# A conv read one input phase later, with two stack tiles, taps built on chip, and blocks moved behind the conv layer norm

## The chip, the cores and the metric

The kernel runs on one core of a Trainium2 chip. The metric is the device time of one execution in microseconds (us), as the median of the runs.

## What is computed

The reference is one inference step of two layers over 288 tokens (256 of a prompt, 8 x 4 of samples). Of a layer, cut to what matters here:

```python
z = x @ w_in                        # columns: u (S5), cv and cg (conv)
y5 = _s5(u, ...)                    # complex diagonal state-space scan, 64 groups
s5_out = gelu(y5) * sigmoid(gelu(y5) @ s5_w_glu)
c = cv * sigmoid(cg)                # GLU
c = causal_dwconv(c, width 31)      # depthwise, per channel; the last 30 rows are an output too
c = silu(layernorm(c))              # over the 1024 conv channels
x = layernorm(ALPHA * x + concat([s5_out, c]) @ w_out)
...                                 # ConvFFN and input embedding, each with a layer norm
```

## The kernel before, in words

Activations lie transposed: 128 channels on the partitions, 288 tokens along the free axis. All weights come as one stream of 128x128 blocks, in the order in which TensorE uses them (`layer_phases`), eight blocks to a unit of 512 KB. SP's queue loads units into four buffers; ScalarE copies each to `whi` (rounded), VectorE makes the remainder `wlo`. Every block is three matmuls of 288 columns (`run`, L373, L378, L379): hi x hi, hi x lo, lo x hi. `next_block` makes the two units that follow the current one ahead of time.

In the mixer of a layer, phase `u0` computes four of the eight S5 inputs u. Then come eight input phases `p0` to `p7` of 32 blocks, each for one chunk of 128 conv channels (its value and its gate). Phases `v0`, `v2` and `v7` of 16 blocks compute u4, u5 and u6; `vz` computes u7. Behind that stand `oc` (the conv half of w_out), `g` (the S5 GLU) and `os` (the other half of w_out).

The conv of chunk j goes this way. `ev` evicts value and gate, and `glu` (VectorE, L144 through a helper that records every VectorE operation) writes their product into `cbuf`, a tile with one buffer that GpSimd's queue has filled with the cached rows (L1117). `cbuf` is stored to a DRAM scratch (`cb_d`, L1138). `stack(j)` then loads the taps `cw` (L1077, 512 KB, mostly zeros: 32 diagonal blocks for each group of 32 channels) and four shifted copies of the chunk back from the scratch into the tile `stack` (L1082, 4 x 282 KB), and stores `cbuf` as output (L1084). `conv(j)` is 64 matmuls of 256 columns (L1107) and 64 of 32 columns (L1110) on 32x32 tiles with `stack` and `cw`. `stack`, `cw` and `cbuf` have one buffer each. Program order is p_j, conv(j-1), stack(j), v_j. GpSimd's queue holds the loads and stores of the conv, some S5 elementwise work (L890 to L940) and the stores of u, y and k of the S5 part; the loads that go with those stores are on SP's queue, between the weights.

The S5 work (`s5`) is a set of generators, stepped between blocks (`tick`). Their waits are lags in an estimate of TensorE's time (`pe_t`, `at`, `wait`), so they set places in program order and not times. For each chunk of eight groups it does: `make_e` (the matrix `em`, L819), `inject` (tile `bu`), a scan on VectorE, `project` (tile `y`), gelu, and two trips through DRAM (`ust`, `u`); `tm` is a matrix that is loaded from DRAM through `k_d`.

Behind `conv(7)`, which follows v7, come four `vz` blocks, then `ln_finish`: statistics on TensorE, a chain of small VectorE operations that ends in `ln_dg`, with the other twelve `vz` blocks as the fill beside it, and a broadcast matmul (L514). Then `c_norm`, `c_silu` and the splits into `xh` (L532) and `xl` feed `oc`, chunk by chunk. `acc_tile` hands out five PSUM banks in turn.

Of the kernel before, what the change touches and what calls it, by code (L numbers as in the profile page):

```python
# [20 lines left out]
DEPTH = 2  # L21
# [32 lines left out]
TICK = 2  # L54
U_LAG = 8000.0
BACK_LAG = 7000.0
LOAD_LAG = 8000.0
# [9 lines left out]
EV_GAP = 10  # L67
HALF_GAP = 6
NATIVE = 10
U_AT = {0: [4], 2: [5], 7: [6]}  # L70
U_END = 7
V_CUT = (0, 4)

# [22 lines left out]
def layer_phases():  # L96
    ph = [("u0", _order("w_in", range(4), range(KD), 4))]
    for j in range(CVC):
        ph.append((f"p{j}", _order("w_in", [8 + j, 16 + j], range(KD), 0)))
        if j in U_AT:  # L100
            ph.append((f"v{j}", _order("w_in", U_AT[j], range(KD), 0)))
    ph.append(("vz", _order("w_in", [U_END], range(KD), 0)))
    ph.append(("oc", _order("w_out", range(KD), range(8, KD), 4)))
    ph.append(("g", _order("s5_w_glu", range(8), range(8), 4)))
    ph.append(("os", _order("w_out", range(KD), range(8), 5)))
    for z, ms in enumerate(EPARTS[:3]):
        ph.append((f"e{z}", _order("pe_w", ms, range(PEK), 0)))
# [12 lines left out]
    ph.append(("pg", _order("pe_w_gate", range(KD), range(KD), 5)))  # L120
    return ph
# [36 lines left out]
class Core:  # L158
# [249 lines left out]
    def ln_acc(self, st, v, last=False):  # L408
# [4 lines left out]
        if i == 0:  # L413
            def mean():
                cps = self.ln_banks(st, 1)[0]
                nc.tensor.matmul(cps[:, :TOK], self.ones_1, v, start=True, stop=True)
                st["c"], st["s1"], st["s2"] = self.ln_tile("ln_c"), self.ln_tile("ln_s1"), self.ln_tile("ln_s2")
                nc.scalar.activation(st["c"], cps[:, :TOK], AF.Copy, scale=1.0 / P)
                st["v0"] = v

            def first():
                self.V.tensor_tensor(v, v, st["c"], OP.subtract)
                nc.scalar.activation(st["s2"], v, AF.Square)
            self.defer(st.get("mean", 2) if st["n"] == DM else MEAN, mean)
            self.defer(2, first)
            return
# [23 lines left out]
    def ln_finish(self, st, fill=None, keep=False, subs=()):  # L450
# [26 lines left out]
        def sub(n=1):  # L477
            while subs and n:
# [29 lines left out]
        y = w  # L508
        dg = self.lp.tile([TG, 3, TG], F32, tag="ln_dg", name="ln_dg", bufs=1)
        V.scalar_tensor_tensor(dg, self.ident[:TG, :TG].rearrange("p (o t) -> p o t", o=1).to_broadcast([TG, 3, TG]),  # L510
                               -1.0, y.rearrange("p (z o) -> p z o", o=1).to_broadcast([TG, 3, TG]),
                               op0=OP.mult, op1=OP.mult)
        fill(1)
        nc.tensor.matmul(b0[:, 8:8 + TOK], self.ones_1[:TG], dg.rearrange("p z t -> p (z t)"),  # L514
                         start=True, stop=True)
# [207 lines left out]

    def stack_tile(self, mp):
        return mp.tile([P, 4, STW], F32, tag="stack", name="stack", bufs=1)


    def s5(self, l, mp):
# [250 lines left out]
        def prep():  # L979
# [7 lines left out]
            for c in range(S5C):  # L987
                while state["i"] < c - 1:
                    yield None
                yield from make_e(*ge)  # L990
                state["e"] = c
                if c + 1 < S5C:
# [62 lines left out]
    def mixer(self, l, ph):  # L1055
        nc, a = self.nc, self.a
        V = self.V
        with self.tc.tile_pool(name="mx", bufs=1) as mp:
# [12 lines left out]
            cst = self.ln_begin(CVC * P)  # L1071
            stacks, cbuf = {}, {}

            def stack(j):
                cb, d = cbuf.pop(j)
                cw = mp.tile([P, 4, 8, 32], F32, tag="cw", name="cw", bufs=1)
                nc.gpsimd.dma_start(cw, a["convw"][l, j])  # L1077
                out = self.stack_tile(mp)

# [4 lines left out]
                nc.gpsimd.dma_start(a["convo"][l, j], cb)  # L1084
                stacks[j] = (out, cw)

# [13 lines left out]
            def conv(j):  # L1100
                st, cw = stacks.pop(j)
                o = self.acc_tile()
# [10 lines left out]
                self.ln_acc(cst, cvo[j], j == CVC - 1)  # L1113

            for j in range(CVC):
                cb = mp.tile([P, CBW], F32, tag="cbuf", name="cbuf", bufs=1)
# [5 lines left out]
                def ev(m, acc):  # L1122
# [17 lines left out]
                    self.defer(2, glu)  # L1140
                self.run(ph[f"p{j}"], self.xs, ev)
                if j:
                    conv(j - 1)
                while "done" not in part:
# [5 lines left out]
            vz = ph["vz"]  # L1150
            vsum = self.sums(vz)
            conv(CVC - 1)
            self.run(vz[V_CUT[0]:V_CUT[1]], self.xs, ev_u, vsum)
            self.flush()
            self.ln_finish(cst, lambda z: z and self.run(vz[V_CUT[1]:], self.xs, ev_u, vsum), keep=True)
            th = {}
# [8 lines left out]
            def c_silu(j):  # L1165
# [3 lines left out]
            self.lazy(self.pipeline(CVC, ((0, lambda j: self.ln_sub(cst, cvo[j])), (1, c_norm), (2, c_silu),  # L1169
                                          (3, lambda j: self.split_lo(8 + j, cvo[j], 0.5)))))  # L1170

            def xs_c(k):
# [36 lines left out]
    def load_p(self, l, mp):  # L1209
        nc = self.nc  # L1210
        self.phi = self.pp.tile([P, PEK, TOK], F32R, name="phi", tag="phi", bufs=1)
        self.plo = self.pp.tile([P, PEK, TOK], F32R, name="plo", tag="plo", bufs=1)
        p32 = mp.tile([P, PEK, TOK], F32, name="p32", tag="sw", bufs=4)
# [123 lines left out]
    def build(self):  # L1337
# [11 lines left out]
        self.ones_d = pp.tile([P, P], F32, name="ones_d")  # L1349
        self.ones_1 = pp.tile([P, P], F32, name="ones_1")  # L1350
        self.ident = pp.tile([P, P], F32, name="ident")
# [8 lines left out]
        nc.vector.memset(self.ones_d, 1.0 / DM)  # L1360
        nc.vector.memset(self.ones_1, 1.0)

        warm = self.lp.tile([P, 1], F32, tag="warm", name="warm", bufs=1)
        nc.scalar.activation(warm, self.ones_1[:, 0:1], AF.Silu)
        make_identity(nc, self.ident)
# [40 lines left out]
def _pack(inp):  # L1406
# [42 lines left out]
    def by_state(names, order):  # L1449
# [5 lines left out]
                        for n in ("state_s5_re", "state_s5_im")], 3)  # L1455
    cw = np.zeros((DEPTH, CVC, 4, 32, 4, 8, 32), np.float32)
    w = np.zeros((DEPTH, 32, CVC * P), np.float32)
    w[:, :CK] = f["conv_w"]
    w = w.reshape(DEPTH, 8, 4, CVC, 4, 32).transpose(0, 3, 2, 5, 4, 1)
    for i in range(32):  # L1460
        cw[:, :, :, i, :, :, i] = w[:, :, :, i]
    o["convw"] = cw.reshape(DEPTH, CVC, P, 4, 8, 32)
    cv = np.zeros((DEPTH, CVC, P, CBW), np.float32)
# [53 lines left out]
```

## Time and profile before

| | us |
|---|---|
| median of 3 runs (2837.29 to 2851.84) | 2843.62 |
| profiled execution | 2835.36 |
| its span, first to last instruction | 2833.5 |
| TensorE busy in the span | 2697.6 |
| VectorE busy | 1820.6 |
| ScalarE busy | 1353.0 |
| GpSimd busy | 303.7 |

The mean granted clock of TensorE over the span is 0.978. The rows further down come from views of the trace: busy time by stretch, waits by engine, the timeline, groups by tile or line. L144 is the line of the helper through which all VectorE operations go, so they are told apart by their tiles. Times in the rows count from the start of the span; layer 0's conv stage is at 61 to 289 us, layer 1's at 1465 to 1694.

### The profile page before, as it was taken

Reading aid. Unit: us, or ns where it says so; the run is one execution under the profiler, and the core shown is the slowest. Engines: PE = TensorE matmul, PEld = TensorE weight load, DVE = VectorE, ACT = ScalarE, POOL = GpSimd, SP = SyncE. Lnnn points to the kernel's source line nnn. Section 1 sums busy time; section 2 is a strip of 40 time slices with the busy share of each in tenths; the row PEclk is TensorE's granted clock in tenths of the full one; section 3 lists DMA queues with packets and bytes.
Section 4 is the critical chain, followed back from the end, with each engine's and each line's share of the span. In section 5 each row is a group of like instructions: output and inputs, shape, how many; then the busy total and the mean of one; then the engine's idle time right before and its main releaser. Section 6 shows DMA issues by size and latency. Waiting matters only on the chain. (4 is left out here: it accounts for less than half of the span.)

```text
span 2833.5 us, 57988 instructions
## 1 busy us (share of the span) xinstructions
PE 2697.6 (95%) x23696; PEld 2634.5 (93%) x23696; DVE 1820.6 (64%) x3049; ACT 1353.0 (48%) x2224; POOL 303.7 (11%) x923
## 2 busy tenths in 40 slices
PE   8887899999999999999998879999999999999997
PEld 7776899999999999999897769999999999999997
DVE  6862778664566446667777537886645664566686
ACT  3442547553455345536364334475534553455363
POOL 3441100100000000000124311010000000000000
PEclk9998999999999999999999989999999999999998
DMA  7977444455454554554468864444554545445543
GB/s 231 252 203 210 147 161 155 160 164 177 159 168 160 182 162 159 174 169 150 158 187 234 226 174 161 160 156 157 173 173 154 171 161 182 161 159 176 166 154 101
DMA packets 175609, 487.72 MB, mean 172 GB/s; under 512 B 37616, under 2 KB 61696, under 8 KB 175344
## 3 DMA queue, kind: packets, MB, share of 16 engines
q1 hardware_dynamic: 160832, 434.56, 47.8%
q0 software_dynamic: 14512, 49.47, 6.4%
q8 instruction: 186, 3.05, 0.4%
q14 instruction: 79, 0.65, 0.1%
HBM read 463.27 MB, written 20.68 MB: 171 GB/s over the span
## 5 line engine op out<-in xcount | busy, mean ns | idle before, releaser
L373 PE MATMUL acc<-xh,whi 128*128 128x288 f32 x4656 | 1390.1, 299 | 14.5 <-ACT xh L532 8.1
L378 PE MATMUL acc<-xl,whi 128*128 128x288 f32 x4325 | 1280.7, 296 | 5.8 <-DVE xl L144 5.3
L379 PE MATMUL acc<-xh,wlo 128*128 128x288 f32 x4325 | 1275.3, 295 | 0.2 <-DVE wlo L144 0.2
L199 ACT ACTIVATE whi<-wraw 128x1024 fp32r<-128x1024 f32 x766 | 792.0, 1050 | 401.1 <-PE acc L378 237.7
L144 DVE TENSOR_TENSOR wlo<-wraw,whi 128x1024 fp32r<-128x1024 f32 x766 | 918.1, 1222 | 45.5 <-ACT whi L199 31.8
L373 PEld LDWEIGHTS acc<-xh,whi 128*128 128x128 f32 x4656 | 877.4, 188 | 20.5 <-ACT xh L532 9.0
L378 PEld LDWEIGHTS acc<-xl,whi 128*128 128x128 f32 x4325 | 814.8, 188 | 10.7 <-DVE xl L144 7.9
L379 PEld LDWEIGHTS acc<-xh,wlo 128*128 128x128 f32 x4325 | 818.0, 189 | 0.5 <-DVE wlo L144 0.5
L373 PE MATMUL acc<-hh,whi 128*128 128x288 f32 x1408 | 416.8, 296 | 0.0
L144 DVE SCALAR_TENSOR_TENSOR fo<-fe,parf,fo 128x304 f32<-128x304 f32 x352 | 188.1, 534 | 354.8 <-ACT fo L1253 348.5
L378 PE MATMUL acc<-hl,whi 128*128 128x288 f32 x1312 | 388.1, 296 | 0.0
L379 PE MATMUL acc<-hh,wlo 128*128 128x288 f32 x1312 | 387.7, 296 | 0.0
L373 PEld LDWEIGHTS acc<-hh,whi 128*128 128x128 f32 x1408 | 265.1, 188 | 0.1
L379 PEld LDWEIGHTS acc<-hh,wlo 128*128 128x128 f32 x1312 | 247.5, 189 | 0.0
L378 PEld LDWEIGHTS acc<-hl,whi 128*128 128x128 f32 x1312 | 247.2, 188 | 0.0
L1249 ACT ACTIVATE fe<-acc 128x256 f32<-128x256 f32 x176 | 67.5, 384 | 308.6 <-PE acc L379 308.6
L1259 POOL COPY fstage<-fe 128x9 f32<-128x9 f32 x176 | 41.8, 237 | 1069.1 <-ACT fe L1250 1064.3
L144 DVE TENSOR_TENSOR x<-x,acc 128x288 f32<-128x288 f32 x96 | 43.3, 451 | 151.3 <-PE acc L379 151.3
L432 ACT ACTIVATE ln_q<-x 128x288 f32<-128x288 f32 x90 | 40.2, 446 | 189.8 <-DVE x L144 189.8
L1253 ACT ACTIVATE fo<-fe,parf 128x304 f32<-128x304 f32 x176 | 112.9, 642 | 17.1 <-ACT fe L1250 0.7
L1107 PE MATMUL acc<-stack,cw 128*32 128x256 f32 x1024 | 79.9, 432 | 40.8 <-DMA stack<-cb_d 35.9
L1273 ACT ACTIVATE hh<-fth 128x288 fp32r<-128x288 f32 x88 | 39.2, 445 | 162.7 <-DVE fth L144 162.7
(237 smaller groups left out, 2373.2 us busy)
## 6 DMA issues: line engine op xcount, KB each, us to landing
wraw<-in_wts_dram SPq DMA_DIRECT2D x776, 512.0 KB
stack<-cb_d POOLq DMA_DIRECT2D x56, 282.0 KB, 9.6
cw<-in_convw_dram POOLq DMA_DIRECT2D x16, 512.0 KB, 6.5
cbuf<-in_convi_dram POOLq DMA_DIRECT2D x16, 283.5 KB, 4.1
cb_d<-cbuf POOLq DMA_DIRECT2D x16, 283.5 KB, 3.4
out_dram<-cbuf POOLq DMA_DIRECT2D x16, 283.5 KB, 11.7
tm<-k_d SPq DMA_DIRECT2D x64, 64.0 KB
sbt<-in_s5b_dram SPq DMA_DIRECT2D x14, 256.0 KB
```

Source lines behind the costliest of these rows:

```text
L144: return f(out, *args, **kw)
L199: self.nc.scalar.activation(hi, self.raw[s], AF.Copy)
L373: nc.tensor.matmul(out, w[0], xh, start=first, stop=False)
L378: nc.tensor.matmul(out, w[0], xl, start=False, stop=False)
L379: nc.tensor.matmul(out, w[1], xh, start=False, stop=last)
L432: nc.scalar.activation(st["q"], v, AF.Square)
L1107: nc.tensor.matmul(o[32 * b:32 * b + 32, :SEQ], cw[:, b, k], st[:, b, 4 * k:4 * k + SEQ], start=(k == 0), stop=False, tile_position=(0, 32 ...
L1249: nc.scalar.activation(e[:, 2:2 + SEQ], acc[:, :SEQ], AF.Copy)
L1253: nc.scalar.activation(o[:, :w], e[:, 2:EW], AF.Identity, bias=self.prm("ffn_conv_b", m), scale=self.prm("ffn_conv_w2", m))
L1259: nc.gpsimd.tensor_copy(stage[:, z, :, 0], e[:, SEQ:EW:6])
L1273: nc.scalar.activation(hh[i], h, AF.Copy, scale=0.5)
```

## The change

Program order becomes p_j, conv(j-2), taps(j-1), stack(j), v_j: the conv of a chunk is read one input phase later. Odd chunks use a second stack tile, which lies in the same memory as phi and plo (needed only after the mixer). The taps are no longer loaded as 512 KB blocks: 16 KB of weights are loaded on SP's queue, and one GpSimd multiply with a 32x32 identity (`eye`) spreads them to `cw`. u4 and u5 are computed after p1 and p3. Setting "matrix em is ready" is put 3 us of estimated TensorE time later. `vz` runs its k in the order 8 to 15, 0 to 7 and is cut in four: four blocks before conv(7), two behind it, six as the fill of `ln_finish`, and four behind the layer norm's first two chunks of normalisation. `ln_dg` shares a tile with `ln_q`, and `ones_1` goes (its users scale by 2048, a power of two). `HALF_GAP`, the least distance in blocks between evictions in `oc` and `os`, goes from 6 to 4.

```diff
+E_LAG = 3000.0
-HALF_GAP = 6
+HALF_GAP = 4
-U_AT = {0: [4], 2: [5], 7: [6]}
+U_AT = {1: [4], 3: [5], 7: [6]}
-V_CUT = (0, 4)
+V_CUT = (4, 6, 12)
...
-    ph.append(("vz", _order("w_in", [U_END], range(KD), 0)))
+    ph.append(("vz", _order("w_in", [U_END], [*range(8, KD), *range(8)], 0)))
...
-        dg = self.lp.tile([TG, 3, TG], F32, tag="ln_dg", name="ln_dg", bufs=1)
+        dg = self.ln_tile("ln_q")[:TG].rearrange("p (z t) -> p z t", z=3)
...
-    def stack_tile(self, mp):
+    def big_tile(self):
+        return self.pp.tile([P, 4 * STW], F32R, tag="big", name="big", bufs=1)
+
+    def stack_tile(self, mp, j=0):
+        if j % 2:
+            return self.big_tile().bitcast(F32).rearrange("p (s w) -> p s w", s=4)
         return mp.tile([P, 4, STW], F32, tag="stack", name="stack", bufs=1)
...
                 yield from make_e(*ge)
-                state["e"] = c
+                self.at(E_LAG, lambda: state.update(e=c))
...
+            def load_w(j):
+                wts[j] = mp.tile([P, 32], F32, tag="cwt", name="cwt", bufs=2)
+                nc.sync.dma_start(wts[j], a["convt"][l, j])
+
+            def taps(j):
+                if j + 1 < CVC:
+                    load_w(j + 1)
+                cws[j] = mp.tile([P, 4, 8, 32], F32, tag="cw", name="cw", bufs=1)
+                shp = [P, 32, 32]
+                nc.gpsimd.tensor_tensor(cws[j].rearrange("p b k o -> p (b k) o"),
+                                        wts.pop(j).rearrange("p (w o) -> p w o", o=1).to_broadcast(shp),
+                                        self.eye.rearrange("p (w o) -> p w o", w=1).to_broadcast(shp), OP.mult)
             def stack(j):
                 cb, d = cbuf.pop(j)
-                cw = mp.tile([P, 4, 8, 32], F32, tag="cw", name="cw", bufs=1)
-                nc.gpsimd.dma_start(cw, a["convw"][l, j])
-                out = self.stack_tile(mp)
+                out = self.stack_tile(mp, j)
...
+            load_w(0)
             for j in range(CVC):
...
                 self.run(ph[f"p{j}"], self.xs, ev)
+                if j > 1:
+                    conv(j - 2)
                 if j:
-                    conv(j - 1)
+                    taps(j - 1)
                 while "done" not in part:
                     self.late.pop(0)[1]()
                 stack(j)
...
+            conv(CVC - 2)
+            taps(CVC - 1)
+            self.run(vz[:V_CUT[0]], self.xs, ev_u, vsum)
             conv(CVC - 1)
             self.run(vz[V_CUT[0]:V_CUT[1]], self.xs, ev_u, vsum)
             self.flush()
-            self.ln_finish(cst, lambda z: z and self.run(vz[V_CUT[1]:], self.xs, ev_u, vsum), keep=True)
+            self.ln_finish(cst, lambda z: z and self.run(vz[V_CUT[1]:V_CUT[2]], self.xs, ev_u, vsum), keep=True)
...
+            self.need(1 - LOOK)
+            self.run(vz[V_CUT[2]:], lambda k: (self.xh[k], self.xl[k]), ev_u, vsum)
...
-        self.phi = self.pp.tile([P, PEK, TOK], F32R, name="phi", tag="phi", bufs=1)
-        self.plo = self.pp.tile([P, PEK, TOK], F32R, name="plo", tag="plo", bufs=1)
+        t = self.big_tile()
+        self.phi, self.plo = [t[:, i * PEK * TOK:(i + 1) * PEK * TOK].rearrange("p (k t) -> p k t", k=PEK)
+                              for i in range(2)]
```

## Rows read from the trace of the kernel before

**Rows 1.** Busy time by stretch: us, busy of each engine, granted clock, DMA share, GB/s.

```profile
61.00:289.17 228.17, 187.66 (x2970) 168.06 (x2970) 138.32 (x250) 85.99 (x158) 76.85 (x137) 0.92 0.80 225
...
360.00:1410.00 1050.00, 1045.60 (x7831) 1042.71 (x7830) 669.18 (x1043) 524.50 (x837) 49.48 (x275) 1.00 0.51 164
...
1464.60:1693.95 229.35, 186.75 (x2975) 167.11 (x2975) 136.12 (x253) 85.03 (x161) 73.74 (x138) 0.92 0.80 220
```

**Rows 2.** Waits of TensorE, 61 to 289: us in total, times, longest.

```profile
PE acc L1107 <- DMA stack<-cb_d: 17.3, 4, 8.1
PE bu L393 <- DMA tm<-k_d: 6.2, 1, 6.2
PE y L393 <- DMA tm<-k_d: 4.6, 1, 4.6
```

**Rows 3.** Waits of TensorE, 1465 to 1694.

```profile
PE acc L1107 <- DMA stack<-cb_d: 18.7, 4, 8.6
PE bu L393 <- ACT em L819: 9.2, 6, 5.5
```

**Rows 4.** Busy time by stretch: an input phase, a conv, a v phase, inject, project.

```profile
210.46:223.55 13.09, 13.04 (x103) 12.80 (x96) 4.46 (x7) 3.25 (x5) 3.30 (x6) 1.00 0.93 248
224.89:229.02 4.13, 4.13 (x129) 3.17 (x129) 1.23 (x1) 1.40 (x3) 1.09 (x2) 1.00 1.01 265
256.69:263.35 6.66, 6.65 (x57) 6.42 (x48) 3.84 (x6) 2.73 (x4) 1.07 (x2) 1.00 0.82 216
165.76:167.10 1.34, 1.34 (x65) 1.16 (x64) 1.34 (x3) 1.34 (x5) 0.00 (x0) 1.00 0.97 293
...
128.18:129.82 1.64, 1.64 (x98) 1.53 (x97) 1.64 (x2) 1.36 (x2) 1.64 (x4) 1.00 0.87 247
```

**Rows 5.** Timeline of VectorE and GpSimd, 229.5 to 256.6: start, us, instruction, [idle before].

```profile
230.47 0.53 DVE L144 SCALAR_TENSOR_TENSOR cbuf<-cvt 128x256 f32<-128x256 f32 x2 [4.28 <-DMA cbuf<-in_convi_dram]
...
255.08 0.53 DVE L144 SCALAR_TENSOR_TENSOR cbuf<-cvt 128x256 f32<-128x256 f32 x2 [9.95 <-DMA cbuf<-in_convi_dram]
...
235.18 2.20 POOL L1082 DMA_DIRECT2D stack<-cb_d  x4 [2.80 <-DMA cb_d<-cbuf]
...
251.78 0.56 POOL L1117 DMA_DIRECT2D cbuf<-in_convi_dram  x1 [13.85 <-DMA out_dram<-cbuf]
```

**Rows 6.** Tile cbuf on VectorE, 40 to 300: durations, first and last start.

```profile
L144 DVE SCALAR_TENSOR_TENSOR cbuf<-cvt x16: 180/324/469, 59.9 to 255.4; 128x256 f32<-128x256 f32 x8, 128x32 f32<-128x32 f32 x8
```

**Rows 7.** DMA issues of the page: count, KB each, median us to landing.

```profile
stack<-cb_d POOLq DMA_DIRECT2D x56, 282.0 KB, 9.6
cw<-in_convw_dram POOLq DMA_DIRECT2D x16, 512.0 KB, 6.5
...
out_dram<-cbuf POOLq DMA_DIRECT2D x16, 283.5 KB, 11.7
```

**Rows 8.** A GpSimd and a VectorE multiply by line or tile: ns min/median/max.

```profile
L895 POOL TENSOR_TENSOR sd<-keep,mag x32: 656/667/1649, 49.9 to 1721.3; 128x288 f32<-128x288 f32 x32
...
L144 DVE TENSOR_TENSOR sw<-sqb,sbt x16: 680/684/1476, 40.9 to 1702.6; 128x512 f32<-128x512 f32 x16
```

**Rows 9.** Busy time by stretch: conv 7, and from its end to the first oc block.

```profile
274.92:289.17 14.25, 10.23 (x85) 9.51 (x78) 8.57 (x26) 7.09 (x14) 1.32 (x3) 1.00 0.25 83
...
269.46:274.92 5.46, 5.46 (x129) 3.45 (x129) 0.00 (x0) 0.00 (x0) 0.00 (x0) 0.74 0.83 306
```

**Rows 10.** Timeline of VectorE and ScalarE in the conv layer norm.

```profile
279.79 0.16 DVE L144 TENSOR_SCALAR ln_ne<-acc 96x6 f32<-96x6 f32 x1 [3.75 <-PE acc L463]
...
282.32 0.46 DVE L144 SCALAR_TENSOR_TENSOR ln_dg<-ident,ln_n 96x288 f32<-96x288 f32 x1
...
291.54 0.43 ACT L532 ACTIVATE xh<-cvo 128x288 fp32r<-128x288 f32 x1
```

**Rows 11.** Waits of TensorE, 289 to 360 (oc).

```profile
PE acc L373 <- ACT xh L532: 4.0, 1, 4.0
PE acc L378 <- DVE xl L144: 3.7, 2, 2.9
```

More of the change, by code (lines that the diff above doesn't have):

```diff
@@ L415, in mean @@
                 cps = self.ln_banks(st, 1)[0]
-                nc.tensor.matmul(cps[:, :TOK], self.ones_1, v, start=True, stop=True)
+                nc.tensor.matmul(cps[:, :TOK], self.ones_d, v, start=True, stop=True)
                 st["c"], st["s1"], st["s2"] = self.ln_tile("ln_c"), self.ln_tile("ln_s1"), self.ln_tile("ln_s2")
-                nc.scalar.activation(st["c"], cps[:, :TOK], AF.Copy, scale=1.0 / P)
+                nc.scalar.activation(st["c"], cps[:, :TOK], AF.Copy, scale=float(DM) / P)
                 st["v0"] = v
@@ L508, in ln_finish @@
         y = w
-        dg = self.lp.tile([TG, 3, TG], F32, tag="ln_dg", name="ln_dg", bufs=1)
+        dg = self.ln_tile("ln_q")[:TG].rearrange("p (z t) -> p z t", z=3)
         V.scalar_tensor_tensor(dg, self.ident[:TG, :TG].rearrange("p (o t) -> p o t", o=1).to_broadcast([TG, 3, TG]),
-                               -1.0, y.rearrange("p (z o) -> p z o", o=1).to_broadcast([TG, 3, TG]),
+                               -float(DM), y.rearrange("p (z o) -> p z o", o=1).to_broadcast([TG, 3, TG]),
                                op0=OP.mult, op1=OP.mult)
         fill(1)
-        nc.tensor.matmul(b0[:, 8:8 + TOK], self.ones_1[:TG], dg.rearrange("p z t -> p (z t)"),
+        nc.tensor.matmul(b0[:, 8:8 + TOK], self.ones_d[:TG], dg.rearrange("p z t -> p (z t)"),
                          start=True, stop=True)
@@ L1071, in mixer @@
             cst = self.ln_begin(CVC * P)
-            stacks, cbuf = {}, {}
+            stacks, cbuf, cws, wts = {}, {}, {}, {}
+            def load_w(j):
[9 more added lines that the diff above has]
+                                        self.eye.rearrange("p (w o) -> p w o", w=1).to_broadcast(shp), OP.mult)
             def stack(j):
                 cb, d = cbuf.pop(j)
-                cw = mp.tile([P, 4, 8, 32], F32, tag="cw", name="cw", bufs=1)
-                nc.gpsimd.dma_start(cw, a["convw"][l, j])
-                out = self.stack_tile(mp)
+                out = self.stack_tile(mp, j)
                 def back(eng):
@@ L1084, in stack @@
                 nc.gpsimd.dma_start(a["convo"][l, j], cb)
-                stacks[j] = (out, cw)
+                stacks[j] = out
             def window(t, b, off):
@@ L1100, in conv @@
             def conv(j):
-                st, cw = stacks.pop(j)
+                st, cw = stacks.pop(j), cws.pop(j)
                 o = self.acc_tile()
@@ L1349, in build @@
         self.ones_d = pp.tile([P, P], F32, name="ones_d")
-        self.ones_1 = pp.tile([P, P], F32, name="ones_1")
         self.ident = pp.tile([P, P], F32, name="ident")
@@ L1360, in build @@
         nc.vector.memset(self.ones_d, 1.0 / DM)
-        nc.vector.memset(self.ones_1, 1.0)
         warm = self.lp.tile([P, 1], F32, tag="warm", name="warm", bufs=1)
-        nc.scalar.activation(warm, self.ones_1[:, 0:1], AF.Silu)
+        nc.scalar.activation(warm, self.ones_d[:, 0:1], AF.Silu)
         make_identity(nc, self.ident)
@@ L1455, in _pack @@
                         for n in ("state_s5_re", "state_s5_im")], 3)
-    cw = np.zeros((DEPTH, CVC, 4, 32, 4, 8, 32), np.float32)
     w = np.zeros((DEPTH, 32, CVC * P), np.float32)
@@ L1459, in _pack @@
     w = w.reshape(DEPTH, 8, 4, CVC, 4, 32).transpose(0, 3, 2, 5, 4, 1)
-    for i in range(32):
-        cw[:, :, :, i, :, :, i] = w[:, :, :, i]
-    o["convw"] = cw.reshape(DEPTH, CVC, P, 4, 8, 32)
+    o["convt"] = w.reshape(DEPTH, CVC, P, 32)
     cv = np.zeros((DEPTH, CVC, P, CBW), np.float32)
```

## The prediction

> **What bounds the kernel now.** I read the stretches first [rows 1]. Behind the conv stage TensorE is busy 1045.6 of 1050 us: there nothing but fewer matmuls would help, and the change takes none away. The two conv stages (61 to 289 and 1465 to 1694) are another matter: 187.7 of 228.2 and 186.8 of 229.4 us busy, at a mean granted clock of 0.92. So 40.5 and 42.6 us stand idle, and part of the busy time runs at 1.2 instead of 2.4 GHz.
>
> The waits of TensorE name the idle time [rows 2, 3]: the stack reload is first in both stages (17.3 and 18.7 us, in four waits each), then the S5 transfers (6.2 and 4.6) and, in layer 1, the matrix `em` (9.2 in six waits).
>
> How much is work? I price the pieces from undisturbed stretches [rows 4]: an input phase of 32 blocks 13.0 us, a conv chunk 4.1, a `v` phase 6.6, an S5 chunk 1.3 + 1.6 = 3. Seven phases, three `v`, the 16 blocks of `vz` (as a `v`), eight convs and six S5 chunks are 91 + 20 + 6.6 + 33 + 18 = 169, with some 4 for the layer norm's matmuls 173. The stage takes 228: 55 us per layer are lost, 40.5 as idle time and the rest to the half clock behind it. That is all that the change can win, about 107 us in two layers.
>
> A second chain runs beside TensorE. `cbuf` has one buffer: GLU j writes it, it goes to DRAM, comes back as the stack, is stored as output, and only when that store has landed may GpSimd's queue load the next `cbuf`, for which GLU j+1 waits on VectorE. One round [rows 5]: GLU at 230.47, stack loads issued at 235.18, next `cbuf` load at 251.78, next GLU at 255.08 after VectorE sat idle for 9.95 us: **24.6 us a round**. TensorE needs 17.1 for such a chunk. From the first GLU to the last are 195.5 us [rows 6], 27.9 per chunk.
>
> **The change part by part.**
>
> *Conv one phase later, two stack tiles.* The stack of j is loaded after p_j as before, but read after p_(j+2) instead of p_(j+1): 17 us more for a load that PE waited for 8 us at most. Its waits (36.0 in both layers [rows 2, 3]) go to zero, but for the last chunk. What is late next is the `cbuf` round, which this part doesn't touch.
>
> *Taps on chip.* Out go 16 loads of 512 KB from GpSimd's queue; 16 loads of 16 KB on SP's queue come in, one phase ahead. In a round that queue moves 512 + 4 x 282 + 2 x 283.5 = 2207 KB [rows 7] in the 21.3 us from GLU to `cbuf` load [rows 5], so 512 KB are 4.9 us of it at this pace; the bounds are 0 (the load runs while the GLU store is still on its way) and 6.5, its whole time to landing [rows 7]. I take 4, nearer to the pace: a round of 20.6.
>
> In come 16 GpSimd multiplies of 128x1024. The nearest rows are 128x288, 0.667 us median and 1.649 at most [rows 8]: by elements 2.4 to 5.9 us. Each waits for the end of conv j-2 (its one `cw` tile), as the load did; behind it in the queue stand the stack loads of j and the S5 stores. The multiply lies in the 4.7 us between GLU and stack issue [rows 5], so I cost its queue time at nothing; without that cover it is 2.4 to 5.9 a round. VectorE can lose time too: its two-input 128x512 multiply takes 0.684 at the median and 1.476 at most [rows 8]. VectorE is busy for 138 of 228 us [rows 1]; bounds 0 and 8 x 5.9 = 47 per layer, I take 3, near the lower end, since wlo is built two units ahead. The Trainium skill ("SBUF — State Buffer", Who interferes with whom) says that a VectorE instruction with two SBUF inputs and a GpSimd one that reads SBUF shut each other out for a whole instruction. The largest values of rows 8 look like that; the rule's price is in a rival.
>
> *Sum up to the last GLU.* TensorE's chunks in the new order, from p_j to p_(j+1), are 16.0 (p, S5), 22.6 (v1), 20.1 (conv 0), 26.7 (conv 1, v3), 20.1, 20.1 and 17.1: 142.7. Seven rounds of 20.6 are 144. The later of the two, chunk by chunk (TensorE to chunk 4, 85.4, then three rounds, 61.8, and 2 for eviction and GLU), gives about 150. On top I keep the S5 transfer waits (10.8 [rows 2]) and 4 for half clock after them: 165 instead of 195.5, a gain of 30.5 per layer.
>
> *E_LAG.* The injection is put 3 us later in TensorE's queue, so other blocks fill the waits for `em`. These waits are not kept in the sum above. The S5 chain has room: VectorE is far from full. Putting u4 and u5 one phase later moves S5 chunks 4 and 5 into phases where VectorE idles; no cost.
>
> *Tail and layer norm.* GLU 7 to conv 7 took 14.4 us (255.08 to 269.46 [rows 5, 9]). Now conv 6 and four `vz` blocks stand in between, and the taps of 7 are built only after conv 6: 2.4 to 5.9 us against a cover of 1.6. With less in the queue I take 14 (12 to 17). Conv 7 takes 4.1 rather than 5.46 at a clock of 0.74 [rows 4, 9]. From its end to the first w_out block were 14.25 us [rows 9]. Two blocks fewer before the statistics, 0.8; the fill falls from 12 blocks to six, 2.5 us, and the VectorE chain that it covers takes 3.0 (279.79 to 282.78 [rows 10]): 2.4 less fill and 0.5 of new wait, 1.9; the last four blocks lie in the 4.0 us wait for `xh` [rows 11]. So 11.6, a gain of 2.7. The tail gains 0.4 + 1.4 + 2.7 = 4.5.
>
> Two costs. `ev_u` of `vz` now stands in ScalarE's queue behind the first normalisations, and the second w_out accumulator takes its bank: the third `xh` ended at 291.97 [rows 10], 2.8 us after w_out's start, so a wait of about 3 there; but this phase is held by VectorE later anyway (3.7 us of `xl` waits [rows 11]), so it hides. S5 chunk 6 comes 4 us sooner relative to w_out and meets that VectorE jam: 2. `HALF_GAP`, `ln_dg` in `ln_q`, `ones_1`, phi and plo in the large tile: nothing on the path.
>
> Per layer: 30.5 + 4.5 - 3 - 2 = 30; two layers 60. The profiled execution took 2835.4 us (span 2833.5) and becomes about 2775; the median of the runs shown lies 8.3 above the profiled one. 2843.6 - 60 = **2784**; with kept waits of 5 to 25 instead of 15, 2764 to 2804.
>
> **The rivals.**
> 1. *The cbuf round keeps its length.* The load left out was hidden in the GLU store's flight, and 24.6 us hold: 7 x 24.6 + 2 + 8 of waits = 182, gain 13.5 + 4.5 - 5 = 13 per layer: 2818. For it: VectorE waits 9.95 us for `cbuf` already [rows 5]. Against: the stack pieces stand behind the 512 KB in one queue. The Trainium skill ("DMA: Bandwidth & Descriptors", Anatomy of one DMA) has about 2 us and bytes by 436 GB/s for a GpSimd DMA: by that 512 KB in the queue are 1.2 us, the round 23.4 and the time, as an estimate, 2802. No run here shows it; the pace above is four times slower.
> 2. *The round shrinks by 6.5 and everything else hides*: TensorE alone sets the pace, 142.7 + 2 + 4 = 149, gain 46.5 + 4.5 - 1 = 50: 2744. Against: DMA share 0.80 over the stage [rows 1], and S5 waits that no edit addresses.
> 3. *The multiply locks VectorE.* If each holds VectorE for its 2.4 us and wlo is late by that: 19 per layer instead of 3: 2816. For: the spread of rows 8. This is the rule on shared ports as a mechanism of this kernel. Against: slack of two units.
> 4. *The wait moves into the queues.* SP and GpSimd loads have lags in estimated TensorE time; with fewer stalls they get less real time, and S5 transfers are awaited for 20 us more per layer: 2824. For: 10.8 us of such waits now.
> 5. *Slower.* The multiply falls behind the GLU store and takes 5.9 us of every round, with no relief from the load left out: 30.5 x 7 = 213.5 against 195.5, with 5 of VectorE and 4.5 of tail gain 18.5 lost per layer: 2880. It decides from 3.3 us a round in which GpSimd is not hidden (27.9 - 24.6). Against: the median row gives 2.4.
>
> That the change doesn't do what it says, is not likely: one tile less to wait for is plain in the order of instructions.
>
> **How the numbers follow.** Forecast 0.44, rival 1 0.20, rival 2 0.13, rival 3 0.08, rival 4 0.09, rival 5 0.06. The range takes in the forecast with its bounds, rivals 1, 3 and 4 and the upper part of 2: 2750 to 2826. A measurement of this kernel can tell some 0.5% (14 us) from no change: faster than 2829 holds for the first five cases but a part of 1 and 4 (their own spread is some 10 us): faster 0.86, same 0.08, slower 0.06.
>
> **What would show it.** Stack waits of TensorE under 8 us in all, and only before conv 7; no `em` waits over 1 us; granted clock over 0.95 in both stages; first to last GLU 155 to 175 us, `cbuf` rounds of 19 to 22 where they bind; GpSimd multiplies of 2 to 5 us, inside the GLU store's flight; from conv 7's end to w_out under 13 us. I am wrong if VectorE waits for `cbuf` as long as before and wlo waits appear at TensorE (rivals 1, 3), or if waits for tm and ust grow (rival 4).

## The result and the profile after

The changed kernel takes 2812.5 us where the kernel before, on the same chip, takes 2842.8: a ratio of 0.9889 (0.9861 to 0.9916). The forecast was 2784, with 60 us of gain; about half of it came. The direction and the range (2750 to 2826) hold, the size does not. The profiled execution fell less than the median, from a span of 2833.5 to 2810.9 us, 22.6, and the trace is read against that.

The waits that were to go are gone. TensorE's waits in the whole profile after (us in total, times, longest):

```profile
PE bu L394 <- ACT em L825: 19.1, 10, 9.4
...
PE kps L863 <- DVE bsm L145: 11.4, 3, 5.7
PE y L394 <- ACT kp L868: 7.4, 1, 7.4
PE acc L376 <- DVE wlo L145: 6.8, 2, 4.5
...
PE acc L1125 <- POOL cw L1090: 3.7, 3, 3.2
PE acc L1125 <- DMA big<-cb_d: 3.3, 1, 3.3
```

The stack reload, 36.0 us before [rows 2, 3], costs 3.3, once, ahead of conv 7; the `tm` waits (10.8 [rows 2]) are no longer in the list. In their place stand four that wait for an engine and not for a transfer: `em`, `bsm`, `kp` and `wlo`, 44.7 us together, three of them operands of S5. The DMA issues of the page after say that the shorter queue is real, 9.6 and 11.7 us before [rows 7]:

```profile
stack<-cb_d POOLq DMA_DIRECT2D x32, 282.0 KB, 7.3
big<-cb_d POOLq DMA_DIRECT2D x24, 282.0 KB, 7.0
...
out_dram<-cbuf POOLq DMA_DIRECT2D x16, 283.5 KB, 9.9
```

The gain can be put in its place with the tile `cbuf` on VectorE (the GLUs; durations, first and last start), layer 0 and layer 1 of the kernel after:

```profile
L145 DVE SCALAR_TENSOR_TENSOR cbuf<-cvt x16: 182/297/628, 59.3 to 246.2; 128x256 f32<-128x256 f32 x8, 128x32 f32<-128x32 f32 x8
...
L145 DVE SCALAR_TENSOR_TENSOR cbuf<-cvt x16: 180/301/427, 1453.6 to 1642.6; 128x256 f32<-128x256 f32 x8, 128x32 f32<-128x32 f32 x8
```

First to last GLU is 186.9 and 189.0 us; before it was 195.5 [rows 6] and, in layer 1, 195.7. That is 8.6 and 6.7 us, where 30.5 a layer were forecast. From the last GLU to the first w_out block the time fell by 3.7 and 5.8 us, where 4.5 were forecast. So one term is missing, and it is the largest. A cut at the fifth GLU shows where. The first four chunks, before and then after (us, busy PE, PEld, DVE, ACT, POOL, granted clock, DMA share, GB/s):

```profile
59.90:181.80 121.90, 105.15 (x1889) 95.39 (x1893) 96.57 (x171) 51.81 (x98) 52.73 (x93) 0.94 0.85 240
1464.30:1583.30 119.00, 100.55 (x1732) 91.15 (x1734) 90.23 (x164) 50.15 (x97) 50.22 (x93) 0.93 0.85 233
```

```profile
59.30:177.30 118.00, 100.10 (x1635) 91.14 (x1637) 96.75 (x160) 49.08 (x92) 51.85 (x91) 0.93 0.82 228
1453.60:1574.90 121.30, 97.99 (x1643) 88.51 (x1645) 90.17 (x153) 49.68 (x96) 55.72 (x92) 0.92 0.74 211
```

The first four chunks gained nothing: 240.9 us before, 239.3 after. Nearly the whole gain of this term is in the last three rounds, from the fifth GLU to the last: 68.6 and 67.4 us, where the kernel before took 73.3 and 76.4.

### The profile page after: what moved, and what is told of

It reads as the page before. It is cut to its first block, busy times and chain, and to the rows that moved or that the text cites. A ratio compares the mean times of both kernels' runs of the same rounds, so it can differ in the third digit from the quotient of the medians.

```text
span 2810.9 us, 57976 instructions
## 1 busy us (share of the span) xinstructions
PE 2690.3 (96%) x23696; PEld 2623.7 (93%) x23696; DVE 1845.6 (66%) x3048; ACT 1352.4 (48%) x2224; POOL 325.8 (12%) x923
## 5 line engine op out<-in xcount | busy, mean ns | idle before, releaser
L379 PE MATMUL acc<-xl,whi 128*128 128x288 f32 x4325 | 1283.7, 297 | 12.9 <-DVE xl L145 12.6
L145 DVE TENSOR_TENSOR wlo<-wraw,whi 128x1024 fp32r<-128x1024 f32 x766 | 921.7, 1227 | 25.6 <-ACT whi L200 11.8
L145 DVE SCALAR_TENSOR_TENSOR fo<-fe,parf,fo 128x304 f32<-128x304 f32 x352 | 188.2, 535 | 345.3 <-ACT fo L1280 339.0
L1276 ACT ACTIVATE fe<-acc 128x256 f32<-128x256 f32 x176 | 67.4, 383 | 286.1 <-PE acc L380 286.1
L433 ACT ACTIVATE ln_q<-x 128x288 f32<-128x288 f32 x90 | 40.1, 446 | 189.9 <-DVE x L145 189.9
L145 DVE SCALAR_TENSOR_TENSOR x<-x,acc 128x288 f32<-128x288 f32 x64 | 28.9, 451 | 124.6 <-PE acc L380 124.6
```

Of the source, the lines that this page charges most:

```text
L145: return f(out, *args, **kw)
L379: nc.tensor.matmul(out, w[0], xl, start=False, stop=False)
L433: nc.scalar.activation(st["q"], v, AF.Square)
L1276: nc.scalar.activation(e[:, 2:2 + SEQ], acc[:, :SEQ], AF.Copy)
```

## Experiments

Two theories stood at the start. **Held queue**: GpSimd works its queue in order; the next `cbuf` load stands in it and waits there until the output store has landed (115.5 us in 14 waits after), and S5's small GpSimd operations, which are queued behind it, come late; ScalarE and VectorE pass that on to TensorE. **Full VectorE**: the multiply on GpSimd shuts VectorE out, and `wlo` and S5 come late for that. The hold in the kernel after:

```profile
POOL cbuf L1136 <- DMA out_dram<-cbuf: 115.5, 14, 12.0
```

The ratios all stand against the kernel before, run on the same chip; a difference of two ratios is uncertain by about 0.004 (10 us). `HALF_GAP`, the shared `ln_dg` tile, `ones_1` and the new order of `vz` were not tried one by one.

| kernel | median us | ratio (95%) | first to last GLU, us |
|---|---|---|---|
| after | 2812.5 | 0.9889 (0.9861 to 0.9916) | 186.9, 189.0 |
| after, store first | 2776.5 | 0.9784 (0.9757 to 0.9811) | 174.9, 175.1 |
| after, taps loaded | 2847.3 | 1.0030 (1.0013 to 1.0047) | 189.3, 194.0 |
| after, no E_LAG | 2810.2 | 0.9895 (0.9868 to 0.9923) | 189.0, 189.9 |
| after, layer norm as before | 2822.8 | 0.9948 (0.9928 to 0.9968) | 187.1, 197.4 |
| before, store first | 2817.4 | 0.9932 (0.9910 to 0.9955) | 193.3, 186.9 |
| before, taps built | 2811.3 | 0.9907 (0.9882 to 0.9932) | 184.6, 182.4 |
| after, store first, taps loaded | 2808.4 | 0.9898 (0.9877 to 0.9918) | 172.9, 182.6 |
| after, store first, short load | 2781.7 | 0.9803 (0.9772 to 0.9834) | 172.4, 174.5 |
| after, store first, multiply twice | 2797.4 | 0.9868 (0.9844 to 0.9893) | 182.3, 188.2 |
| before, taps built, store first | 2789.9 | 0.9825 (0.9799 to 0.9850) | 176.1, 174.3 |
| after, S5 blocks as before | 2807.9 | 0.9898 (0.9880 to 0.9916) | 188.0, 186.9 |
| after, conv order as before | 2797.0 | 0.9859 (0.9835 to 0.9883) | 186.8, 187.5 |

**The output store ahead of the stack loads** (on the kernel after).

```diff
-                back(nc.gpsimd if j < CVC - 1 else nc.sync)
                 nc.gpsimd.dma_start(a["convo"][l, j], cb)
+                back(nc.gpsimd if j < CVC - 1 else nc.sync)
```

> The changed kernel, with the output store of cbuf issued before the four stack loads instead of behind them; nothing else differs. Held queue (my theory): in the changed kernel GpSimd's in-order queue stands for 115.5 us before the cbuf loads, waiting for that store to land behind 1.1 MB of stack; S5 work behind it comes late, and ScalarE and VectorE, in order too, pass the delay on (TensorE waits for em 19.1, bsm 11.4, kp 7.4, wlo 6.8). So GpSimd's cbuf waits fall under 40 us, those four waits of TensorE (44.7 in all) under 20, first to last GLU from 186.6 and 188.7 us to under 172, the time from 2812 to 2775-2790. Rival, full VectorE: the multiply locks VectorE and S5 fills it (busy 133 of 187 us): GpSimd's wait falls as well, but the four waits stay, and the time is 2805-2815.

It took 2776.5 us, 36 less than the changed kernel by the medians and 30 by the ratios: the fastest of all kernels in the table. The time and the hold (16.7 us) came as expected; the four waits, expected under 20, are 20.3, and first to last GLU, expected under 172, is 175. GpSimd's hold and the waits of TensorE behind it fell together:

```profile
POOL cbuf L1136 <- DMA out_dram<-cbuf: 16.7, 7, 4.0
```

```profile
PE bu L394 <- ACT em L825: 9.7, 10, 2.6
...
PE y L394 <- ACT kp L868: 4.9, 3, 3.3
...
PE kps L863 <- DVE bsm L145: 3.4, 2, 3.0
...
PE acc L376 <- DVE wlo L145: 2.3, 1, 2.3
```

Of 44.7 us 20.3 are left. The multiplies are all still there, so full VectorE does not explain the 24.4 that went; what the 20.3 come from, this run does not say.

The swap also brings the next `cbuf` load forward, so a shorter `cbuf` round is a rival. Up to the fifth GLU the time fell by 7.3 and 7.8 us (118.0 to 110.7, 121.3 to 113.5), in the last three rounds by 4.8 and 6.2 (to 63.9 and 61.2). In layer 0 neither VectorE waits for a `cbuf` load nor TensorE for a stack before the fifth GLU, in either of the two kernels, so those 7.3 us are not the round's. In layer 1 VectorE waits 5.2 us once before the fifth GLU, and 0.7 with the store first; there, and in the last rounds, the swap can have worked through the round as well.

How a hold gets to TensorE is seen in one place of the kernel after: the timelines of GpSimd, ScalarE, VectorE and TensorE around 1527 us (start, us, instruction, [idle before and what ended it]).

```profile
1518.00 0.58 POOL L1102 DMA_DIRECT2D out_dram<-cbuf  x1
1527.26 0.56 POOL L1136 DMA_DIRECT2D cbuf<-in_convi_dram  x1 [8.68 <-DMA out_dram<-cbuf]
1527.81 0.36 POOL L936 COPY hin<-h 128x32 f32<-128x32 f32 x2
...
1528.87 0.66 POOL L897 TENSOR_TENSOR stb<-stb,quart 128x288 int32<-128x288 int32 x1
...
1529.57 0.68 ACT L903 ACTIVATE stb<-stb 128x576 f32<-128x576 int32 x1 [10.86 <-POOL stb L897]
...
1530.49 1.32 ACT L825 ACTIVATE em<-sw,mask 128x512 f32<-128x512 f32 x2
...
1530.62 0.48 DVE L145 SCALAR_TENSOR_TENSOR yw<-yw,y 128x288 f32<-128x288 f32 x1 [9.71 <-ACT yw L968]
...
1531.25 0.46 PE L394 MATMUL bu<-ust,em 128*32 128x72 f32 x4 [9.36 <-ACT em L825]
```

GpSimd stands 8.68 us in front of the `cbuf` load. Right behind it come `hin` and `stb`, each under 1 us; ScalarE has waited 10.86 us for `stb`, the next `em` stands behind that on ScalarE, and TensorE has stood for 9.36. The wait of one DMA issue goes almost whole from GpSimd to ScalarE and on to TensorE.

**The taps loaded again** (on the kernel after: the load of 512 KB in the place of the multiply, no 16 KB loads).

```diff
-                nc.gpsimd.tensor_tensor(cws[j]..., wts.pop(j)..., self.eye..., OP.mult)
+                nc.gpsimd.dma_start(cws[j], a["convw"][l, j])
```

> The changed kernel, with the taps loaded as 512 KB blocks on GpSimd's queue, at the place of the multiply; nothing else differs. Held queue: 512 KB more stand before the stack loads and the cbuf store, which lands later by 2 to 5 us a round; GpSimd's cbuf waits grow from 115.5 to 140-160 us and the time to 2820-2835. Full VectorE: without 16 multiplies of 2 us that lock it out, VectorE gains 30 us and the time falls to 2795-2810.

At 1.0030 the change without its multiply gains nothing at all. The hold came as expected for the held queue (140.9 us), the time did not: 2847.3 lies above both ranges. The waits of TensorE name a part of the 35 us (0.0141 by ratio, 40); "issue" is time in which it waited for nothing that the profile shows:

```profile
PE acc L1116 <- DMA cw<-in_convw_dram: 17.3, 2, 9.1
...
PE acc L1116 <- issue: 11.5, 3, 6.2
```

With one `cw` tile the load can only begin when one conv has ended, and the next conv reads it. Where that hurts, the timeline of TensorE shows: all of these waits but 0.5 us stand at conv 6 and conv 7, behind the last GLU. In layer 1:

```profile
1663.78 1.08 PE L1116 MATMUL acc<-stack,cw 128*32 128x256 f32 x8 [9.15 <-DMA cw<-in_convw_dram]
...
1677.43 1.08 PE L1116 MATMUL acc<-big,cw 128*32 128x256 f32 x8 [6.15 <-issue]
```

From the last GLU to the first w_out block the loaded taps take 40.0 and 37.7 us, the built ones 30.4 and 28.5: 18.9 of the 22.8 us by which the two profiled spans differ. Up to the fifth GLU they cost nothing (117.6 and 119.5 us against 118.0 and 121.3). Full VectorE, which would have made the loaded taps faster, falls as the main cause.

**The injection without its lag.**

```diff
-                self.at(E_LAG, lambda: state.update(e=c))
+                state["e"] = c
```

> The changed kernel, with em marked ready at once, as in the kernel before (no 3 us of lag). If the lag does its work, the waits for em grow from 19.1 us by some 3 us in each of ten places: 40 us and a time of 2822-2835. If em is late because ScalarE is held by the S5 tables behind GpSimd's queue, the lag hardly matters: em waits 20-30 us, time 2810-2820.

2810.2 against 2812.5: nothing. The `em` waits are 17.1 us without the lag and 19.1 with it, where either theory expected 20 or more; the lag does not touch what makes `em` late.

**The layer norm's blocks as before.**

```diff
-V_CUT = (4, 6, 12)
+V_CUT = (0, 4, 16)
...
-            self.run(vz[:V_CUT[0]], self.xs, ev_u, vsum)
...
-            self.need(1 - LOOK)
-            self.run(vz[V_CUT[2]:], lambda k: (self.xh[k], self.xl[k]), ev_u, vsum)
```

> The changed kernel, with the vz blocks placed as in the kernel before: none between conv 6 and conv 7, four behind conv 7, twelve as the fill, none behind the layer norm. If the new places are worth what the trace shows around the layer norm, conv 7 waits 1.6 us longer for its taps and from its end to the first w_out block pass 14 us instead of 11.8 per layer: 6 to 9 us more, 2818-2822. Rival: w_out is held by the xl splits on VectorE a few blocks later anyway, and the time is 2810-2815.

It costs 10 us by the medians (2822.8, where 2818 to 2822 was expected), 17 by the ratios. The stretch from the end of conv 7 to the first w_out block, here and then in the kernel after:

```profile
262.21:276.35 14.14, 10.12 (x78) 9.39 (x78) 8.57 (x26) 7.10 (x14) 1.32 (x3) 1.00 0.30 105
```

```profile
264.46:276.28 11.82, 8.81 (x67) 7.97 (x66) 7.31 (x25) 5.13 (x11) 0.00 (x0) 0.98 0.14 46
```

The same stretch in layer 1 is 14.14 us here too, and 11.82 in the kernel after. So 2.3 us a layer are shown in the tail. The rest of the difference lies in layer 1 ahead of it (197.4 against 189.0 from GLU to GLU), where this edit changes nothing that I can name; it stays open.

**The store first, on the kernel before**, the same swap of two lines.

> The kernel before with one edit: the output store of `cbuf` is issued ahead of the stack loads instead of behind them. Held queue (GpSimd's queue stands in the `cbuf` load until the output store has landed; 154.8 us in 14 waits in the kernel before): the waits fall under 80 us and S5 work behind them comes sooner, but the stack, which this kernel reads one phase earlier and already waits 36 us for, now stands behind 283 KB more: part of the gain is given back; 2805 to 2830, stack waits of TensorE 36 to 50. Rival, the stack reload was the bound of the kernel before: stack waits grow by 4 us and more a chunk in most of 16 chunks, 2845 to 2890.

0.9932, 19 us. The hold in the kernel before, then the hold and the stack waits here:

```profile
POOL cbuf L1117 <- DMA out_dram<-cbuf: 154.8, 14, 13.8
```

```profile
POOL cbuf L1117 <- DMA out_dram<-cbuf: 51.4, 11, 7.2
```

```profile
PE acc L1107 <- DMA stack<-cb_d: 32.8, 8, 6.1
```

The stack waits were 35.9 us in the kernel before: they did not grow, though 36 to 50 were expected. The held queue was in the kernel before too.

**The taps alone, on the kernel before** (the multiply at the place of the load, ahead of the stack loads of the same chunk).

```diff
-                nc.gpsimd.dma_start(cw, a["convw"][l, j])
+                nc.gpsimd.tensor_tensor(cw..., wts.pop(j)..., self.eye..., OP.mult)
```

> The kernel before with one part of the change alone: the taps are built by GpSimd from 16 KB loads, conv order, stack tile and layer norm as before. If the 512 KB loads are what the round pays for: the stack lands 3 to 4 us sooner, its waits of 36 us at TensorE fall under 20, the round falls by 2 to 4 us, 2795 to 2822. Rival, the multiply only pays when the conv is a phase later, since here it stands directly ahead of the stack loads in GpSimd's queue and begins only when the conv before has ended: 2835 to 2850, stack waits of 30 us or more.

0.9907, 26 us: nearly what the whole change gives. First to last GLU fell by 10.9 and 13.3 us, more than with the whole change. The stack waits are still 27.6; "under 20" was a miss, and the time fell anyway. From the last GLU to the first w_out block nothing changed (34.1 and 33.8 us, before 34.1 and 34.3): in the old order the loaded taps cost nothing there, where in the new order they cost most.

**Both, on the kernel after: store first and taps loaded.**

> The changed kernel with the output store ahead of the stack loads (2776.5 with taps built on chip), and with the taps loaded as 512 KB again. In the changed kernel the loads cost 34.9 us. If these came from a longer hold of GpSimd's queue: with the store first they cost under 12, 2776 to 2788, and the waits of the `cbuf` load stay under 50 us. If they come from the bytes themselves, wherever the store stands: 2795 to 2815, with waits of TensorE for `cw` of 10 us or more.

0.9898 against 0.9784: the loads cost 0.0114 (32 us) with the queue free (24.6 us of hold), so their price is not the hold. That they would cost under 12 us fell; the other branch, the bytes themselves, has the time (2808.4), and `cw` waits just under the 10 us it asked for. TensorE waits for the taps themselves, and again nearly all of it at conv 6 and conv 7:

```profile
PE acc L1116 <- issue: 10.0, 3, 7.0
PE acc L1116 <- DMA cw<-in_convw_dram: 9.8, 2, 7.7
```

**Store first and a shorter `cbuf` load** (only the columns that the GLU leaves).

```diff
-                nc.gpsimd.dma_start(cb, a["convi"][l, j])
+                nc.gpsimd.dma_start(cb[:, 30 + SEQ:], a["convi"][l, j, :, 30 + SEQ:])
+                nc.gpsimd.dma_start(cb[:, :30], a["convi"][l, j, :, :30])
```

> The changed kernel with the output store ahead of the stack loads (2776.5), and the `cbuf` load cut to the columns that the GLU does not write (311 of 567 columns, two DMAs; 128 KB less of 283.5 a chunk). By the price of the taps (34.9 us for 16 x 496 KB) 16 x 128 KB are worth 9 us: 2764 to 2770, VectorE's `cbuf` waits of 20.0 us under 12. Rival, the round is no longer on the path once the store goes first: 2773 to 2780, whatever VectorE waits for `cbuf`.

VectorE's wait for that load is as good as gone, and the time is not better: 0.9803 against 0.9784, within the uncertainty. The wait with the store first, then with the shorter load:

```profile
DVE cbuf L145 <- DMA cbuf<-in_convi_dram: 20.0, 3, 10.9
```

```profile
DVE cbuf L145 <- DMA cbuf<-in_convi_dram: 1.2, 2, 0.6
```

Once the store goes first, the `cbuf` load is no longer the bound: in its place VectorE's waits for ScalarE's `cvt` before the GLU grew from 9.1 to 15.0 us. 128 KB less in each load bought nothing there.

**Store first and each multiply done twice** (work added, the same result written again).

```diff
+                nc.gpsimd.tensor_tensor(cws[j]..., wts[j]..., self.eye..., OP.mult)
                 nc.gpsimd.tensor_tensor(cws[j]..., wts.pop(j)..., self.eye..., OP.mult)
```

> The changed kernel with the output store ahead of the stack loads (2776.5), and each of the 16 multiplies on GpSimd done twice (work added, 16 x 1.97 us): the price of the multiply. Locked VectorE: in the changed kernel the VectorE instructions that run beside a multiply are stretched (a 128x288 accumulate of the conv layer norm from 0.45 to 2.17 us, a `wlo` split from 1.22 to 3.73 at most); if TensorE pays for each, 16 more cost 20 to 32 us, 2796 to 2808. Rival, the units built ahead and the cover in GpSimd's queue hide them: 2774 to 2784, with the same stretches in the trace.

0.9868 against 0.9784: 0.0084, 24 us by the ratios and 21 by the medians, 1.3 to 1.5 us for each of 16 more multiplies that last 1.9 to 2.8 us (median 2.0). So a second multiply is not hidden; that the first costs as much is not shown. TensorE's waits have grown by its own operand and by S5's:

```profile
PE bu L394 <- ACT em L825: 16.7, 10, 5.1
...
PE acc L1128 <- POOL cw L1093: 9.7, 4, 2.7
PE kps L863 <- DVE bsm L145: 7.6, 2, 4.1
```

How much of it is GpSimd's queue and how much VectorE's lost time, these runs don't separate.

**Taps and store first, on the kernel before.**

> The kernel before with the taps built on chip (alone 2811.3) and the output store ahead of the stack loads (alone 2817.4), conv order, stack tile and layer norm as before. The changed kernel with the store first is 2776.5, of which 10 to 12 are the blocks behind the layer norm. If the later conv and the second stack tile are worth their waits (27.6 us for the stack in the kernel with the taps alone) once GpSimd's queue is not held: 2802 to 2815 here, stack waits of TensorE 22 us or more. Rival, the later conv gives nothing even then: 2782 to 2793, the two edits add up (18 and 24 us).

0.9825: the two edits add up (0.0068 + 0.0093 = 0.0161, measured 0.0175). The rival's range (2782 to 2793) holds. The kernel after with the store first, 0.9784, is 0.0041 ahead of it, and undoing the layer norm's blocks cost 0.0059. For the later conv and the second stack tile nothing is left that these runs could tell from zero.

**The S5 blocks as before.**

```diff
-U_AT = {1: [4], 3: [5], 7: [6]}
+U_AT = {0: [4], 2: [5], 7: [6]}
```

> The changed kernel (2812.5) with one part undone: the input blocks of S5 chunks 4 and 5 stand behind phases 0 and 2 again instead of 1 and 3. The taps alone on the kernel before gave 2811.3 and the layer norm's blocks are worth 10, so the later conv and these blocks together lost about 11 us. If the S5 chunks moved into later phases are what loses it (they meet the eviction and GLU work and the held queue there): 2796 to 2805, TensorE's waits for `em`, `bsm`, `kp` and `wlo` fall from 44.7 to under 32. Rival, it is the held queue wherever these chunks stand: 2806 to 2820, the same waits at other places.

0.9898 against 0.9889: no difference. `em`, `bsm` and `kp` together are still 43.9 us, at other places. The rival holds.

**The conv order as before** (on the kernel after).

```diff
-                if j > 1:
-                    conv(j - 2)
                 if j:
-                    taps(j - 1)
+                    conv(j - 1)
+                taps(j)
...
-            conv(CVC - 2)
-            taps(CVC - 1)
             self.run(vz[:V_CUT[0]], self.xs, ev_u, vsum)
```

> The changed kernel (ratio to before 0.9889, 2812.5) with the conv order alone undone: conv j stands behind phase j+1 again, its taps built ahead of its stack loads; the two stack tiles stay, as do the taps on chip, the layer norm's blocks, S5's blocks and the injection. As forecast (the later conv takes 36 us of stack waits off TensorE): these waits come back, 20 to 30 us of them, and the time grows, 2820 to 2840. Rival (by the ratios of the parts the taps alone give 0.0093 of the time and the layer norm's blocks 0.0059, together 0.0152, more than the whole change's 0.0111): the later conv gives nothing or loses, because S5 and the `cbuf` round are late in place of the stack; 2795 to 2812, with 20 us or more of stack waits and `em`, `bsm`, `kp` and `wlo` waits under 30 us instead of 44.7.

0.9859 against 0.9889: no slower; the 8 us that it is faster by the ratios lie within the uncertainty. GpSimd's hold and TensorE's waits:

```profile
POOL cbuf L1136 <- DMA out_dram<-cbuf: 108.9, 12, 11.6
```

```profile
PE acc L1125 <- DMA stack<-cb_d: 17.8, 4, 5.5
PE acc L1125 <- DMA big<-cb_d: 11.8, 4, 4.5
...
PE bu L394 <- ACT em L825: 8.3, 6, 4.7
```

The stack waits are back, 29.6 us of them, and the `em` waits halve; those for `bsm`, `kp` and `wlo` fall from 25.6 to 2.9. First to last GLU is 186.8 and 187.5, as with the later conv. This is an exchange of waits. The hold is nearly that of the kernel after (115.5), so a hold does not make TensorE wait for S5 by itself: it does once nothing else stops TensorE first. That both waits hide behind one late chain is how I read it; no run shows the chain by itself.

## Why the prediction was half right

**What bounds the kernel now.** The loss of 55 us a layer was read rightly (for two layers its own numbers give 111 us, not 107; nothing hangs on it). Its ordering by TensorE's waits was not a ranking by worth: the longest item, 36 us of stack reload, was worth nothing by itself (conv order as before). In the first four chunks, which decide, the stack is only 1.6 and 4.4 us of the idle time before (layer 0, layer 1); most of its waits stand in the last rounds, where the `cbuf` round can bind:

```profile
PE acc L1107 <- DMA stack<-cb_d: 1.6, 1, 1.6
```

```profile
PE acc L1107 <- DMA stack<-cb_d: 4.4, 2, 2.6
```

**Conv a phase later.** "Its waits go to zero, but for the last chunk" holds to the letter (3.3 us, once). "What is late next is the `cbuf` round" was right for the last rounds alone.

**Taps on chip.** The round's relief was forecast at 4 us, from 24.6 to 20.6. The last round of the kernel after is 20.9 us (GLU at 225.0, next at 245.9), 20.7 in layer 1: right, and rival 1, the round that stays, falls. With the taps loaded again this round is 23.8 and 23.5, so 2.8 to 2.9 of the relief are the taps'. What the loaded taps cost behind the last GLU in the new order, 9 us a layer, the prediction did not see: it priced them by the round alone.

**The multiply.** 2.4 to 5.9 us were estimated by elements; it took less:

```profile
L1090 POOL TENSOR_TENSOR cw<-cwt,eye x16: 1902/1926/2127, 85.2 to 1652.8; 128x1024 f32<-128x1024 f32 x16
```

Its price was probably too low: 3 us a layer for VectorE and nothing for the queue, but 8 more multiplies a layer cost 10 to 12 us. If the first set costs what the second does, which no run shows, 7 to 9 us a layer are missing here; they would lie within the missing time that is split below, not on top of it. Part of it is visible on VectorE. The accumulate of the conv layer norm, and the `wlo` split, by tile (ns min/median/max), layer 0 after:

```profile
L145 DVE TENSOR_TENSOR cvo<-cvo,ln_c x7: 447/1736/2170, 132.5 to 254.2; 128x288 f32<-128x288 f32 x7
```

```profile
L145 DVE TENSOR_TENSOR wlo<-wraw,whi x33: 1197/1218/3728, 59.8 to 246.4; 128x1024 fp32r<-128x1024 f32 x33
```

An instruction of 0.45 us becomes one of 2.17 where a multiply runs beside it. The `wlo` of 3.73 us and its multiply:

```profile
126.91 3.73 DVE L145 TENSOR_TENSOR wlo<-wraw,whi 128x1024 fp32r<-128x1024 f32 x1
127.61 1.93 POOL L1090 TENSOR_TENSOR cw<-cwt,eye 128x1024 f32<-128x1024 f32 x1
```

The multiply ends at 129.54 and `wlo` 1.10 us later, nearly its whole usual time of 1.22. The Trainium skill ("SBUF — State Buffer", Who interferes with whom) says that a VectorE instruction with two SBUF inputs and a GpSimd one that reads SBUF exclude each other for the whole instruction; the trace agrees as to VectorE, which stands until the multiply has ended, while the multiplies stay at 1.90 to 2.13 us. Rival 3 is right as a mechanism; if the first set costs what the second does, at 10 to 12 us a layer instead of 19.

**The sum up to the last GLU** is the step that failed. Forecast were 85.4 us of TensorE to the fifth GLU, 61.8 + 2 for the last rounds, 10.8 of kept waits and 4 for half clock: 164 (165 as rounded there). Measured in layer 0: 118.0 us to the fifth GLU, of which 100.1 busy at a mean clock of 0.93. That is, as an estimate (busy time by the clock), 93 of work and 7 for half clock, and 17.9 idle; the three rounds take 68.6. In layer 1: 90 of work, 8, 23.3 idle, and 67.4. So of the 23 to 25 us that are missing per layer

- 8 and 5 are work that the sum of pieces left out. In layer 0 six injections and four projections stand ahead of the fifth GLU, not four of each (2.6), four `kps` groups of 0.43, the statistics of the first conv (0.75) and the start of conv 2 (2);
- 10 and 16 are idle time and half clock above the 14.8 kept. What I kept were waits for `tm`, and they vanished; `em` (5.9 and 13.2), `kp` (7.4 in layer 1), `wlo` (4.5 and 2.2) and `bsm` (3.5 in layer 0) came in their place. The sentences that failed are "These waits are not kept in the sum above. The S5 chain has room: VectorE is far from full". Room on VectorE is no room when the chain passes through GpSimd's queue: with that queue freed the four waits fell from 44.7 to 20.3 us;
- 5 and 4 are the rounds: only the last one or two run at the pace of the round.

With the store first the rounds come to the forecast, and the idle time comes near the waits that were kept:

```profile
57.60:168.30 110.70, 96.88 (x1663) 87.97 (x1662) 96.84 (x159) 49.17 (x92) 53.82 (x91) 0.97 0.89 244
1440.50:1554.00 113.50, 99.51 (x1642) 89.99 (x1644) 91.39 (x153) 50.10 (x96) 54.19 (x92) 0.94 0.82 225
```

By the same estimate that is 94 of work in both layers, 3 and 6 for half clock, 14 idle (14.8 were kept for the last two together), and then rounds of 63.9 and 61.2 us, where 63.8 were forecast. The work, 85.4, was too low there as well.

**E_LAG and U_AT.** Undoing either changes nothing, so "no cost" holds, and the gain hoped for from E_LAG (no `em` waits over 1 us) did not come: the longest is 9.4. Nor did a granted clock over 0.95: the first four chunks have 0.93 and 0.92.

**Tail and layer norm.** Forecast 14.25 to 11.6 us from conv 7's end to w_out; measured 11.82. The sum of the tail, 4.5 a layer, met 3.7 and 5.8. This part was worked out from instruction to instruction, and held. The cost of 2 us a layer in w_out is of the right size: from the first w_out block of layer 0 to layer 1's first GLU the time grew by 2.1 us, and from layer 1's first w_out block to the end by 0.6. The `xl` waits of the whole profile grew from 5.3 to 12.6 us, those for `xh` fell from 8.1 to 4.7.

**The rivals.** The second, TensorE alone, 2744, falls. Rival 4 put the missing gain in "the wait moves into the queues", right in kind, but named SP's and GpSimd's loads and their lags; it is GpSimd's compute instructions behind one held DMA issue. Its sign for recognition, more waits for `tm` and `ust`, did not appear. Rival 5, slower, asked for a multiply that costs 3.3 us a round and more with no relief from the load left out; the second set cost 1.3 to 1.5 us each, and the relief came.

The parts don't add up: undone one at a time they come to 0.0141 (taps), 0.0059 (layer norm) and -0.0030 (conv order), 0.017 together, and the change gives 0.0111. With the conv order of before, the taps give 0.0093, and with the later conv 0.0141; the difference is little more than the uncertainty, but the traces show a place for it. In the old order the stretch behind the last GLU takes the same time with loaded and with built taps (34 us); in the new one, where convs 6 and 7 stand in it, loaded taps make it 9 us longer per layer. With the store first the same comparison gives 0.0107 and 0.0114, so the ratios do not show that the later conv makes loaded taps dearer.

## What to carry to other kernels

A DMA issue that waits for a landing on an engine with an in-order queue is a wait of everything queued behind it, tiny instructions for other stages included: look for the longest wait in each issuing queue, and issue the transfer it waits for first. Rank an engine's waits by what is late right behind them and not by their length: 36 us of stack waits were removed for no gain that the runs could tell from zero, and a swap of two lines that TensorE's waits did not point to brought 30 to 36. A sum of pieces needs every engine that an operand passes through, a nearly idle one too.

## What was not expected of the hardware

GpSimd's 128x1024 multiply takes 1.93 us, where scaling its 128x288 row by elements gives 2.4; but a VectorE instruction with two inputs in SBUF beside it grows from 0.45 to 2.17 us, by nearly the length of the multiply. And 128 KB less in each of 16 loads (store first, short load) brought nothing at a DMA share of 0.8 to 0.9, while the place of a transfer in the queue brought 30 us.
